# The last 40 adaLN rows: multiplied on GpSimd and summed on ScalarE, in place of one VectorE instruction

## The chip, the cores and the metric

The kernel runs on one core of one Trainium2 chip. A core has five engines that take their instructions in order, each from its own queue, and wait for one another by semaphores: TensorE (PE: matrix multiplies, with the weight loads listed apart as PEld), VectorE (DVE), ScalarE (ACT), GpSimd (POOL) and SyncE (SP), which here issues the DMAs. Times are microseconds (us) on the device, for one execution of the whole kernel; the figure for a kernel is the median of its runs.

## The reference, cut to what matters

One block of a transformer for 256 tokens of width 2048, all in float32: an FFN, a mixer (differential attention beside a causal convolution), and a second FFN. Each of the three has a norm in front whose scale and shift come from a vector `c` (adaLN), and a gate behind.

```python
c_act = silu(c)                                       # 1 x 2048
ada = einsum('bd,de->be', c_act, w_ada) + b_ada       # 1 x 18432: nine vectors of 2048
sh1, sc1, g1, shm, scm, gm, sh2, sc2, g2 = split(ada, 9)
h = modulate(rms_norm(x, ffn1_norm), sh1, sc1)        # h * (1 + sc) + sh
x = x + 0.5 * g1 * swiglu(h, ffn1_w_gu, ffn1_w_down)
h = modulate(rms_norm(x, mix_norm), shm, scm)
x = x + gm * hybrid_mixer(h, ...)
h = modulate(rms_norm(x, ffn2_norm), sh2, sc2)
x = x + 0.5 * g2 * swiglu(h, ffn2_w_gu, ffn2_w_down)
```

`ffn1_w_gu` and `ffn2_w_gu` are 2048 x 11264, the `w_down` 5632 x 2048, `w_ada` is 2048 x 18432 (151 MB, the largest input).

## The kernel before, in words

**adaLN rows.** The 18432 outputs of the adaLN product are 144 "rows" of 128. A row is a tile of 128 partitions (its outputs) by 2048 elements (the input dimension), 1 MB. The function `ada(j)` (L185) loads row j into a buffer `raw` by a DMA on SP (L190), multiplies it by `c_bc`, the activated `c` on all partitions, and sums along the free axis into one column of `ada_cols` by one instruction on VectorE (L191); that instruction shows in the profile as two, CUSTOM_DVE_ANT_0 and DVE_READ_ACCUMULATOR2_ANT. After each odd row a small add puts the bias on two columns (L195). Rows 0 to 47 belong to the first FFN, 48 to 95 to the mixer, 96 to 143 to the second FFN. Within 48, 32 alternate scale and shift for the 16 blocks of the norm, and the last 16 are the gate. `modulation` (L226) turns a pair into the scale and shift for one block (L233), and calls for rows that haven't come yet; `gate` (L258) does so for the last 16.

**Weights.** `w_tile` (L286) loads a weight tile of 128 x 2048 (1 MB) into the same four `raw` buffers, on the same SP queue (L292). Each half of it is split in two: ScalarE casts it to `whi` (L303), VectorE subtracts to get the rest, `wlo` (L305). `whi` and `wlo` have four buffers each, that is two weight tiles. `mm3` (L324) makes a product out of three matmuls (L327, L331, L332).

**Second FFN.** `ffn` (L637) first runs stage A: for each of 22 column chunks it loads the weight tile for the first quarter of the input, multiplies it for both token halves, and ScalarE copies the accumulators away (L664). Its later tiles take the other three quarters, for which the norm's blocks 4 to 15 must be done (`piece`, `complete`, L425 and L438; instructions L447 to L452), and so rows 104 to 127. Between the tiles the code asks for rows: 0.78 of a row per tile in stage A up to row 128 (`ada_share`, L215, called at L655, L770 and L774), then 0.5 a tile up to row 144 (L859), with `ada_until` (L200) where a block's rows are due. The first call in the second FFN (L769) stands in `tc.issue_after(st.last.ins)`, which queues what it traces on the engine of that instruction, VectorE, behind it. Then come the tiles of the down product, in a Strassen-like form (L463), whose gate needs rows 128 to 143.

**Order.** In the source, loads, splits, matmuls and rows are only stated; a planner orders each engine's queue by the order of the source and its own estimate of what is ready, and puts in the semaphore waits. A DMA into a `raw` buffer waits until the buffer's last reader is done. GpSimd has little: memsets and the reciprocal roots of the norms (L152, an exponent of -0.5). Before the second FFN starts, the mixer's end adds the residual (L1334, L1335), sums squares (L358), takes the root (L152) and runs the first block of the norm (L384 to L403).

Of the kernel before, what the change touches and what calls it, by code (L numbers as in the profile page):

```python
# [20 lines left out]
AF = mybir.ActivationFunctionType  # L21
ALU = mybir.AluOpType
# [18 lines left out]
EXT = (1,) * 8 + (2,) * 4 + (3,) * 3  # L41
LOADS = [(0,), (1,), (2, 3), (4, 5), (6, 7)] + [(c,) for c in range(8, NCH)]
BY_TILE = 5
X_BEHIND = 2
AGAIN = [4, 5, 6]
EARLY = [[3, 8, 9], [4, 5, 6], [7, 10, 11], [12, 13, 14]]
# [34 lines left out]
def block_kernel(ctx: ExitStack, tc: tile.TileContext, x_in, pos_in, w_ada, small, w_gu1, w_dn1,  # L81
                 w_in, w_out, w_gu2, w_dn2, out):
    nc = tc.nc
# [14 lines left out]
    def nm(s):  # L98
        uid[0] += 1
        return f"{s}_{uid[0]}"  # L100
# [40 lines left out]
    c_bc = cbp.tile([P, D], F32, tag="c_bc", name="c_bc")  # L141
# [41 lines left out]
    ada_cols = {}  # L183

    def ada(j):  # L185
        g = j // 8
        if g not in ada_cols:
            ada_cols[g] = const.tile([P, 8], F32, name=f"ada{g}")
        raw = rawp.tile([P, D], F32, tag="raw", name=nm("raw"))
        nc.sync.dma_start(out=raw, in_=w_ada[j])  # L190
        nc.vector.tensor_tensor_reduce(out=raw, in0=raw, in1=c_bc, scale=1.0, scalar=0.0, op0=ALU.mult,  # L191
                                       op1=ALU.add, accum_out=ada_cols[g][:, j % 8:j % 8 + 1])
        if j % 2 == 1:
            p0, o = _COLS["bada"][0] + j - 1, j % 8 - 1
            nc.vector.tensor_add(out=ada_cols[g][:, o:o + 2], in0=ada_cols[g][:, o:o + 2], in1=cst[:, p0:p0 + 2])  # L195
# [4 lines left out]
    def ada_until(j):  # L200
        while ada_next[0] < j:
            ada(ada_next[0])
            ada_next[0] += 1
# [11 lines left out]
    def ada_share(r, limit):  # L215
        credit[0] += r
        while credit[0] >= 1.0:
            credit[0] -= 1.0
            if ada_next[0] < limit:
                ada(ada_next[0])  # L220
                ada_next[0] += 1
# [88 lines left out]
    def w_first(cs, held):  # L310

        n = len(cs)
        raw = blk([P, 2, 512])
        w_dma[0] = nc.sync.dma_start(out=raw[:, :n, :], in_=w_gu1[cs[0]:cs[0] + n, 0].rearrange("c p n -> p c n")[:, :, :512])
        hi = blk([P, 2, 512], F32R) if held else whp.tile([P, 2, 512], F32R, tag="whi", name=nm("whi"))
        lo = blk([P, 2, 512], F32R) if held else wlp.tile([P, 2, 512], F32R, tag="wlo", name=nm("wlo"))

        def split():
            nc.scalar.copy(out=hi[:, :n, :], in_=raw[:, :n, :])  # L319
            nc.vector.tensor_sub(out=lo[:, :n, :], in0=raw[:, :n, :], in1=hi[:, :n, :].bitcast(F32))  # L320

        return [lambda j, i=i: (hi[:, i, :], lo[:, i, :]) for i in range(n)], split
# [314 lines left out]
    def ffn(st, w_gu, w_dn, gate_base, ada_a, ada_b, nxt, again, early, early_3):  # L637
# [37 lines left out]
        if not st.done:  # L675
# [4 lines left out]
            def load(i):  # L680
                cs = LOADS[i]
                if ext[cs[0]] == 1:
                    views, split = w_first(cs, X_BEHIND < i < BY_TILE)
                    ws.update(zip(cs, views))
                    if i < BY_TILE:
                        return split
                    split()
                else:
                    ws[cs[0]] = w_tile(w_gu[cs[0], 0], False, (0, ext[cs[0]]), ext[cs[0]] < 4)

            def begin_ready():
                while begun[0] < 4 and base + 2 * begun[0] + 2 <= ada_next[0]:
                    st.tile(st.raws[begun[0]], tmp([P, S]), (begun[0], slice(0, S)))
                    begun[0] += 1
# [10 lines left out]
            split = []  # L705
            for i in range(BY_TILE):
                split.append(load(i))
                if i == X_BEHIND:
                    with tc.issue_after(w_dma[0].ins):
# [7 lines left out]
            def products(i, t):  # L717
                for c in LOADS[i]:
                    acc = acc_tile()
                    mm3(acc, act(0, t), ws[c](0), True, True, i > 0 and t == 0)  # L720
                    if parts[c] is None:
                        parts[c] = blk([P, NT, 512])
                    last_part[0] = nc.scalar.copy(out=parts[c][:, t, :], in_=acc)

            with tc.manual_schedule(engines={mybir.EngineType.Activation, mybir.EngineType.DVE, mybir.EngineType.PE}):
# [17 lines left out]
                products(4, 0)  # L743
                for i in range(BY_TILE):
                    products(i, 1)
                    if i == 2:
                        load(BY_TILE)
                    if i == 3:
                        begin_ready()
            for i in range(BY_TILE, len(LOADS) + AHEAD):  # L750
                if i < len(LOADS):
# [704 lines left out]
```

## Time and profile before the change

| | |
|---|---|
| median of 3 runs | 1838.04 us (1837.12 to 1838.94) |
| the profiled execution, first to last instruction (its span; it has no other time) | 1835.9 us |
| TensorE busy | 1812.0 us |
| VectorE busy | 1521.8 us |
| ScalarE busy | 960.7 us |
| GpSimd busy | 28.3 us, 29 instructions |
| L191, the 142 whole rows on VectorE | 324.1 us, 2.28 us each |

A row of the timeline gives the start and the duration in us, the engine, the line of the kernel, the operation, the tiles it writes and reads, their shapes and a count (x2 where neighbours are merged); in square brackets stands how long the engine had been idle before it, and what it had waited for. A row of a group gives the total in us, the mean of one in ns, and the idle time ahead. A row of waits gives who waited for whom: the total in us, how often, and the longest. A row of windows gives the stretch and its length, then busy time and number of instructions (x) for each engine, the granted clock of TensorE, the busy share of the DMA engines and GB/s; where it is asked for one line alone, that line's engine only. A line like "min/median/max" gives durations in ns.

### The profile page before, as it was taken

Reading aid. Unit: us, or ns where it says so; the run is one execution under the profiler, and the core shown is the slowest. Engines: PE = TensorE matmul, PEld = TensorE weight load, DVE = VectorE, ACT = ScalarE, POOL = GpSimd, SP = SyncE. Lnnn points to the kernel's source line nnn. Section 1 sums busy time; section 2 is a strip of 40 time slices with the busy share of each in tenths; the row PEclk is TensorE's granted clock in tenths of the full one; section 3 lists DMA queues with packets and bytes.
Section 4 is the critical chain, followed back from the end, with each engine's and each line's share of the span. In section 5 each row is a group of like instructions: output and inputs, shape, how many; then the busy total and the mean of one; then the engine's idle time right before and its main releaser. Section 6 shows DMA issues by size and latency. Waiting matters only on the chain.

```text
span 1835.9 us, 22042 instructions
## 1 busy us (share of the span) xinstructions
PE 1812.0 (99%) x8205; PEld 1493.1 (81%) x8205; DVE 1521.8 (83%) x2018; ACT 960.7 (52%) x1477; POOL 28.3 (2%) x29
## 2 busy tenths in 40 slices
PE   7999999999999999999999999999999999999998
PEld 5788888888888887888888788888888888888887
DVE  7889869999888787898999768878877755699877
ACT  6554344444444343566798646664444444455453
POOL 0000000000000000000110000000000000000000
PEclk9999999999999999999999999999999999999999
DMA  9988978889899888765544467899777755555552
GB/s 375 352 307 300 352 272 301 343 306 340 336 322 357 353 343 329 289 256 187 181 159 161 161 229 294 315 335 339 263 273 284 285 197 188 184 206 208 205 210 111
DMA packets 72731, 495.93 MB, mean 270 GB/s; under 512 B 8192, under 2 KB 8624, under 8 KB 15152
## 3 DMA queue, kind: packets, MB, share of 16 engines
q1 hardware_dynamic: 72624, 494.53, 72.2%
q8 instruction: 64, 1.05, 0.2%
q14 instruction: 43, 0.35, 0.1%
HBM read 492.37 MB, written 2.12 MB: 269 GB/s over the span
## 4 chain that ended last, share of the span: by engine, by line
PE 90%; DVE 5%; ACT 2%; issue 1%; DMA 1%; POOL 0%; SPq 0%; POOLq 0%; DVEq 0%; ACTq 0%
PE acc L331 28%; PE acc L332 28%; PE acc L327 28%; DVE wlo L305 2%; PE tp L836 1%; PE tp L332 1%; PE tp L331 1%; PE tp L327 1%; DMA blk<-in_w_gu_dram 1%; PE acc L1123 1%; DVE blk L1015 1%; ACT whi L303 0%; PE tp L392 0%; DMA blk<-in_w_ada_dram 0%; DVE wlo L511 0%
## 5 line engine op out<-in xcount | busy, mean ns | idle before, releaser
L303 ACT CAST whi<-raw 128x1024 fp32r<-128x1024 f32 (+1 forms) x581 | 599.8, 1045 | 610.8 <-PE acc L332 450.3
L331 PE MATMUL acc<-wlo,blk 128*128 128x512 f32 x2340 | 913.5, 390 | 5.8 <-DVE wlo L305 5.8
L327 PE MATMUL acc<-whi,blk 128*128 128x512 f32 x2343 | 913.3, 393 | 1.7 <-ACT blk L401 1.3
L332 PE MATMUL acc<-whi,blk 128*128 128x512 f32 x2340 | 912.5, 390 | 0.1
L305 DVE TENSOR_TENSOR wlo<-raw,whi 128x1024 fp32r<-128x1024 f32 (+1 forms) x581 | 692.6, 1210 | 210.3 <-ACT whi L303 208.8
L331 PEld LDWEIGHTS acc<-wlo,blk 128*128 128x128 f32 x2340 | 439.6, 188 | 99.4 <-DVE wlo L305 10.3
L327 PEld LDWEIGHTS acc<-whi,blk 128*128 128x128 f32 x2343 | 440.0, 188 | 92.8 <-ACT blk L401 1.7
L332 PEld LDWEIGHTS acc<-whi,blk 128*128 128x128 f32 x2340 | 439.3, 188 | 92.4 <-DVE blk L403 0.7
L191 DVE CUSTOM_DVE_ANT_0 raw<-raw,c_bc 128x2048 f32<-128x2048 f32 x142 | 324.1, 2284 | 9.0 <-DMA raw<-in_w_ada_dram 8.8
L510 ACT CAST whi<-raw 128x1024 fp32r<-128x1024 f32 (+1 forms) x56 | 53.0, 946 | 70.2 <-PE tp L332 31.9
L511 DVE TENSOR_TENSOR wlo<-raw,whi 128x1024 fp32r<-128x1024 f32 (+1 forms) x56 | 60.9, 1088 | 19.0 <-ACT whi L510 18.7
L664 ACT COPY blk<-acc 128x512 f32<-128x512 f32 x72 | 41.9, 589 | 60.6 <-PE acc L332 57.9
L1015 DVE SCALAR_TENSOR_TENSOR blk<-blk,cst,blk 128x245 f32<-128x245 f32 (+21 forms) x176 | 70.5, 456 | 0.6 <-ACT blk L1013 0.5
L828 DVE TENSOR_TENSOR blk<-acc,blk 128x512 f32<-128x512 f32 x88 | 56.8, 682 | 0.2
L327 PE MATMUL acc<-blk,blk 128*128 128x512 f32 x104 | 41.3, 400 | 1.0 <-ACT blk L319 1.0
L332 PE MATMUL acc<-blk,blk 128*128 128x512 f32 x100 | 39.0, 392 | 0.0
L331 PE MATMUL acc<-blk,blk 128*128 128x512 f32 x100 | 39.0, 390 | 0.0
L830 DVE TENSOR_TENSOR blk<-blk 128x256 f32<-128x256 f32 x88 | 33.3, 417 | 0.7 <-ACT blk L829 0.7
L829 ACT ACTIVATE blk<-blk 128x256 f32<-128x256 f32 x88 | 32.2, 411 | 2.1 <-DVE blk L828 2.1
L349 DVE TENSOR_TENSOR blk<-tp,blk 128x512 fp32r<-128x512 f32 x44 | 29.9, 684 | 1.6 <-ACT blk L348 1.6
L305 DVE TENSOR_TENSOR blk<-raw,blk 128x1024 fp32r<-128x1024 f32 x24 | 28.8, 1218 | 0.8 <-ACT blk L303 0.8
L450 ACT ACTIVATE tmp<-tp,ada,scales 128x128 f32<-128x128 f32 x36 | 14.8, 459 | 28.0 <-DVE scales L233 15.5
(223 smaller groups left out, 1023.5 us busy)
## 6 DMA issues: line engine op xcount, KB each, us to landing
raw<-in_w_gu_dram SPq DMA_DIRECT2D x161, 1024.0 KB, 5.3
raw<-in_w_ada_dram SPq DMA_DIRECT2D x142, 1024.0 KB, 6.3
raw<-in_w_dn_dram SPq DMA_DIRECT2D x88, 1024.0 KB, 5.2
raw<-in_w_in_dram SPq DMA_DIRECT2D x40, 1024.0 KB, 4.8
raw<-in_w_out_dram SPq DMA_DIRECT2D x16, 1024.0 KB, 4.8
raw<-in_w_gu_dram SPq DMA_DIRECT2D x8, 768.0 KB, 6.0
blk<-in_w_gu_dram SPq DMA_DIRECT2D x10, 512.0 KB, 14.5
blk<-gate_line SPq DMA_DIRECT2D x6, 512.0 KB, 4.9
```

The costliest lines, as they stand in the source:

```text
L191: nc.vector.tensor_tensor_reduce(out=raw, in0=raw, in1=c_bc, scale=1.0, scalar=0.0, op0=ALU.mult, op1=ALU.add, accum_out=ada_cols[g][:, j ...
L303: nc.scalar.copy(out=hi[:, :m, :], in_=rw)
L305: nc.vector.tensor_sub(out=lo[:, :m, :], in0=rw, in1=hi[:, :m, :].bitcast(F32))
L327: nc.tensor.matmul(acc, ah, wh, start=start, stop=False)
L331: nc.tensor.matmul(acc, ah, wl, start=False, stop=False)
L332: return nc.tensor.matmul(acc, al, wh, start=False, stop=stop)
L510: nc.scalar.copy(out=hi[:, :n, :], in_=src)
L511: nc.vector.tensor_sub(out=lo[:, :n, :], in0=src, in1=hi[:, :n, :].bitcast(F32))
L664: last_part[0] = nc.scalar.copy(out=parts[c][:, t, :], in_=accs[t])
L828: nc.vector.tensor_add(out=p[:, t, :], in0=accs[t], in1=p[:, t, :])
L830: nc.vector.tensor_mul(out=p[:, t, 256:], in0=p[:, t, :256], in1=p[:, t, 256:])
L1015: nc.vector.scalar_tensor_tensor(out=y[:, d:], in0=u, scalar=w, in1=y[:, d:], op0=ALU.mult, op1=ALU.add)
```

## The change

For rows 104 to 143, the two lines of VectorE's multiply-and-sum become a GpSimd multiply of the whole tile in place, and a copy on ScalarE, also in place, whose accumulator gives the sum along the free axis. Rows up to 103 stay as they were. The bias add stays on VectorE, and the load stays where it was.

```diff
+ON_POOL = 104
...
         raw = rawp.tile([P, D], F32, tag="raw", name=nm("raw"))
         nc.sync.dma_start(out=raw, in_=w_ada[j])
-        nc.vector.tensor_tensor_reduce(out=raw, in0=raw, in1=c_bc, scale=1.0, scalar=0.0, op0=ALU.mult,
-                                       op1=ALU.add, accum_out=ada_cols[g][:, j % 8:j % 8 + 1])
+        dst = ada_cols[g][:, j % 8:j % 8 + 1]
+        if j < ON_POOL:
+            nc.vector.tensor_tensor_reduce(out=raw, in0=raw, in1=c_bc, scale=1.0, scalar=0.0, op0=ALU.mult,
+                                           op1=ALU.add, accum_out=dst)
+        else:
+            nc.gpsimd.tensor_tensor(out=raw, in0=raw, in1=c_bc, op=ALU.mult)
+            nc.scalar.activation(out=raw, in_=raw, func=AF.Copy, accum_out=dst)
         if j % 2 == 1:
             p0, o = _COLS["bada"][0] + j - 1, j % 8 - 1
             nc.vector.tensor_add(out=ada_cols[g][:, o:o + 2], in0=ada_cols[g][:, o:o + 2], in1=cst[:, p0:p0 + 2])
```

## The prediction

> **What bounds the kernel now.** I read the page first, then busy time by stage, then the groups of VectorE and ScalarE in the stage that the change reaches, then the waits of TensorE and of the DMA queue, then single rows of the timeline.
>
> ```profile
> span 1835.9 us, 22042 instructions
> PE 1812.0 (99%) x8205; PEld 1493.1 (81%) x8205; DVE 1521.8 (83%) x2018; ACT 960.7 (52%) x1477; POOL 28.3 (2%) x29
> ```
> ```profile
> L191 DVE CUSTOM_DVE_ANT_0 raw<-raw,c_bc x40: 2277/2284/2293, 1115.4 to 1458.3; 128x2048 f32<-128x2048 f32 x40
> L191 DVE DVE_READ_ACCUMULATOR2_ANT ada<- x40: 77/82/85, 1117.6 to 1460.5; 128x1 f32 x40
> ```
> ```profile
> core 0: us, PE busy (x) PEld busy (x) DVE busy (x) ACT busy (x) POOL busy (x), PEclk, DMA share, GB/s
> 1115.00:1180.00 65.00, 65.00 (x295) 53.68 (x294) 54.92 (x64) 38.28 (x55) 0.00 (x0) 1.00 0.85 329
> 1180.00:1260.00 80.00, 80.00 (x356) 65.98 (x355) 66.89 (x76) 43.79 (x57) 0.00 (x0) 1.00 0.93 340
> 1260.00:1360.00 100.00, 100.00 (x458) 82.65 (x457) 80.95 (x96) 47.63 (x62) 0.00 (x0) 1.00 0.76 283
> 1360.00:1460.00 100.00, 100.00 (x454) 82.77 (x453) 78.11 (x90) 44.57 (x54) 0.00 (x0) 1.00 0.77 283
> ```
> ```profile
> PE tp L392 <- DVE tmp L384: 0.9, 2, 0.6
> ```
>
> The kernel is bound by TensorE, which is busy 99% of the span. The 40 rows that move are the ones multiplied between 1115 and 1460 us, in the second FFN; there TensorE is busy in every microsecond at the full granted clock (PEclk 1.00), and the last line is its only wait on another engine between 1100 and 1470 us: 0.9 us. VectorE is 80 to 85% busy there, yet it makes nothing late. So relief for VectorE has next to nothing to win: at most that 0.9 us. What decides is whether the new path of a row makes TensorE late. I count 0.2% of the time, 3.7 us, as the least that a measurement of this kernel can tell from no change.
>
> **What goes and what comes.** VectorE loses, for each row, 2.28 us of multiply-and-sum and 0.08 us of accumulator read: 40 x 2.37 = 95 us, none of it on the path to the end. Added are one GpSimd multiply of 128x2048 and one ScalarE pass with accumulator per row. The bias add (L195) stays on VectorE, but now waits for ScalarE. No DMA moves, but each row's buffer is released later.
>
> GpSimd's price. No row shows a large multiply on it; the nearest are these (the first line is a memset of one element per partition):
>
> ```profile
> 0.24 0.10 POOL L1446 MEMSET const-float32-0.0<- 128x1 f32 x1 [0.24 <-issue]
> 881.77 0.95 POOL L1064 MEMSET blk<- 64x1024 f32 x1
> 20.23 0.56 POOL L152 TENSOR_TENSOR rstd<-rstd,half 128x1 f32<-128x1 f32 x1 [8.82 <-DVE rstd L151]
> ```
>
> One stream costs (0.95 - 0.10) / 1023 = 0.83 ns an element, so 1.70 us for 2048, and the smallest two-operand instruction 0.56 us. The multiply has three streams, two read and one written: fully overlapped it is 0.56 + 1.70 = 2.3 us, with two in turn 4.0, all three in turn 5.7. I take 4.5, nearer to two in turn, because the memset row shows the write side alone and two operands have to come in beside it. The Trainium skill (GPSIMD Engine Reference, Elementwise — side-by-side cycle accounting) gives 4497 ns, measured, for an fp32 add of 2048 elements; no run here shows it yet, and by it the sum would be the one below.
>
> Whether it runs beside VectorE. The trace of before has GpSimd instructions that meet a VectorE instruction with two operands in SBUF:
>
> ```profile
> 998.19 1.21 DVE L305 TENSOR_TENSOR wlo<-raw,whi 128x1024 fp32r<-128x1024 f32 x1
> 998.36 1.92 POOL L152 TENSOR_TENSOR rs<-rs,half 128x4 f32<-128x4 f32 x1 [37.51 <-DVE rs L151]
> ```
> ```profile
> 1013.98 1.21 DVE L305 TENSOR_TENSOR wlo<-raw,whi 128x1024 fp32r<-128x1024 f32 x1
> 1014.15 1.91 POOL L152 TENSOR_TENSOR rs<-rs,half 128x4 f32<-128x4 f32 x1 [6.65 <-DVE rs L151]
> 1018.55 1.14 POOL L152 TENSOR_TENSOR rs<-rs,half 128x4 f32<-128x4 f32 x1 [2.49 <-DVE rs L151]
> ```
>
> The same 128x4 instruction takes 1.91 us in two cases and 1.14 us in a third. In both long cases it started 0.17 us after an L305 and ended 0.88 us after that L305 ended (998.19 + 1.21 = 999.40, against 1000.28; 1015.19 against 1016.06). So a VectorE instruction that reads two SBUF operands holds GpSimd off until it is done. The other direction can't be seen, since these GpSimd instructions read almost nothing; its bounds are that a multiply holds VectorE off for 0 us and for its whole 4.5. I take the whole: it is the same pair of instructions wanting the same way into the memory, and nothing shown makes the way divisible. The Trainium skill (SBUF — State Buffer, Who interferes with whom) states just this rule: a VectorE instruction with two SBUF inputs and a GpSimd instruction that reads SBUF shut each other out, whichever starts first, for the whole instruction. The trace agrees for VectorE first (0.88 us both times); GpSimd first, no run here shows, and without the rule the sum would be that of the first rival.
>
> **The sum, 1115 to 1260 us (145 us).** These are VectorE's groups there, and its L191 time by stage:
>
> ```profile
> L305 DVE TENSOR_TENSOR wlo<-raw,whi 128x1024 fp32r<-128x1024 f32 x52 | 61.5, 1220 | 20.7 <-ACT whi L303 20.7
> L191 DVE CUSTOM_DVE_ANT_0 raw<-raw,c_bc 128x2048 f32<-128x2048 f32 x22 | 50.1, 2283 | 0.0
> L784 DVE TENSOR_TENSOR blk<-acc,blk 128x512 f32<-128x512 f32 x6 | 3.8, 681 | 0.0
> L447 DVE TENSOR_SCALAR tmp<-tp,scales,ada 128x128 f32<-128x128 f32 x10 | 3.6, 406 | 1.9 <-PE tp L392 1.8
> ```
> ```profile
> 1115.00:1180.00 65.00, 25.05 (x22) 1.00 0.85 329
> 1180.00:1260.00 80.00, 25.21 (x22) 1.00 0.93 340
> 1260.00:1360.00 100.00, 20.18 (x17) 1.00 0.76 283
> 1360.00:1460.00 100.00, 20.50 (x19) 1.00 0.77 283
> ```
>
> VectorE is busy 54.9 + 66.9 = 121.8 us, of which L191 is 50.3, so 71.5 us stay. Of these 7.4 us (L784 and L447) read PSUM and at most one SBUF tensor, and can run beside GpSimd; 64 us can't. The 22 rows need 22 x 4.5 = 99 us of GpSimd. What excludes each other is 64 + 99 = 163 us in a stage of 145: 18 us too much. At 2.3 us a multiply it is 115 us and fits; at 4.0 it is 152 (7 over); at 5.7 it is 189 (44 over).
>
> How much of that is hidden:
>
> ```profile
> 1128.02 1.27 ACT L664 COPY blk<-acc 128x512 f32<-128x512 f32 x2 [2.83 <-PE acc L332]
> 1129.19 2.00 ACT L303 CAST whi<-raw 128x1024 fp32r<-128x1024 f32 x2
> 1130.27 2.36 DVE L305 TENSOR_TENSOR wlo<-raw,whi 128x1024 fp32r<-128x1024 f32 x2 [0.97 <-ACT whi L303]
> 1133.46 1.27 ACT L664 COPY blk<-acc 128x512 f32<-128x512 f32 x2 [2.28 <-PE acc L332]
> ```
>
> A weight tile takes TensorE 5.44 us (from one L664 pair to the next). The halves split at 1130.27 to 1132.63 are for the tile that TensorE begins about when the next L664 pair starts, at 1133.5: VectorE is ahead by some 2 us for the first half and, as the second half is wanted 2.7 us later, 3.6 us for the second. That lead, 3 us, is paid back once. So the stage grows by 18 - 3 = 15 us, all of it TensorE waiting for L305.
>
> From 1260 to 1460 us: VectorE 159.1 - 40.7 = 118.4 us without L191, and 18 rows x 4.5 = 81; together 199.4 of 200 even if everything excludes. It fits; I count 0, and at 5.7 us a multiply (221 us) up to 20.
>
> The first rows.
>
> ```profile
> 1081.58 24.36 SPq L190 DMA_DIRECT2D raw<-in_w_ada_dram  x3
> ```
>
> The first of them is loaded from 1081.6 us on, yet multiplied only at 1115.4 (row of L191), because the code (L769) queues the multiply behind the last norm instruction, which is VectorE's. GpSimd isn't VectorE, so a multiply may start earlier and hold up the residual adds or the reciprocal root (L152) between 1095 and 1110 us, where TensorE does wait (the 0.9 us above); that costs 0 to 4.5 us, and it takes two multiplies out of the crowded stage, worth up to 9. I count 0.
>
> ScalarE. Its pass:
>
> ```profile
> L358 ACT ACTIVATION_READ_ACCUMULATOR tmp<-xall x20: 184/186/190, 6.7 to 1107.9; 128x1 f32 x20
> L451 ACT CAST blk<-tmp 128x512 fp32r<-128x512 f32 x4 | 2.4, 625 | 0.0
> L303 ACT CAST whi<-raw 128x1024 fp32r<-128x1024 f32 x52 | 52.4, 1050 | 12.4 <-DMA raw<-in_w_gu_dram 11.5 <-DVE ada L191 0.5 <-PE acc L332 0.3
> ```
>
> From 512 to 1024 elements the cast grows by 0.425 us, so 2048 are 1.05 + 0.85 = 1.9, with the accumulator read 2.1 us. In the stage ScalarE is busy 38.3 + 43.8 = 82.1; with 22 x 2.1 = 46 it is 128 of 145. It fits if it doesn't wait: 17 us are spare, 0.77 us a row.
>
> Forecast: 15 us on the profiled span, 1835.9 + 15 = 1851. The median of the three runs, 1838.04, is 2.1 us above that span, so the time is 1853 us.
>
> **Rivals.** First, not slower: GpSimd yields, or holds VectorE only while it starts. Then VectorE drops to 71.5 of 145 us, ScalarE has its 17 us to spare, a later row costs nothing, and the time stays at 1838, no more than 1 us below. For it: no row shows VectorE held off, and at under 3.7 us a multiply (64 + 22 x 3.7 = 145) everything fits even under full exclusion. That is the point from which it decides. Against: the rows at 998 and 1014. Chance 0.24, of which 0.02 for over 0.2% faster.
>
> Second, the queue of ScalarE. The pass waits for the multiply, and behind it in order stand the accumulator copies (L664) and the casts of the next tile. If the planner puts it so that ScalarE waits half a multiply, 2.25 us, a row, 22 x (2.25 - 0.77) = 33 us are added, in place of the 15: 1871. It decides from 0.77 us of wait a row. For it: ScalarE's spare time lies in a 2.3 us gap per tile ahead of L664, hardly over the 2.1 us that the pass takes. Against: ScalarE waits for DMA or VectorE before its casts for 12 us in this stage without TensorE noticing. Chance 0.12.
>
> Third, the four load buffers.
>
> ```profile
> SPq L292 <- DVE ada L191: 106.3, 23, 6.2
> ```
>
> Weight loads wait for rows' buffers to come free: 106 us over 23 loads between 1100 and 1470 us. A row will hold its buffer 4.5 + 2.1 - 2.37 = 4.2 us longer, and the load that takes the buffer next starts that much later.
>
> ```profile
> raw<-in_w_gu_dram SPq DMA_DIRECT2D x63, 1024.0 KB, 6.0
> ```
> ```profile
> 1204.92 0.33 SPq L292 DMA_DIRECT2D raw<-in_w_gu_dram  x1
> ```
> ```profile
> 1213.67 1.99 ACT L303 CAST whi<-raw 128x1024 fp32r<-128x1024 f32 x2
> ```
>
> A load issued at 1204.92 lands 6.0 us later, at 1210.9, and is cast at 1213.67: 2.8 us to spare. 4.2 - 2.8 leaves 1.4 us late; for half of the 22 rows' loads that is 15 us, less the 3 us of lead 12: 1850. It decides from a hold of 2.8 us more, that is from a multiply of 3.1 us. For it: ScalarE waits 11.5 us for such landings already (row of L303). Against: landing gets shorter where loads are spread out. Chance 0.10. The forecast has 0.54.
>
> **How the numbers follow.** Slower is forecast, second and third rival: 0.76. Same is 0.22, faster 0.02. The low end is no change less 1 us, 1837. The high end is a multiply of 5.7 us: 44 - 3 = 41 us over, 1879, which also takes in the second rival at 1871; beyond lies the sum of 5.7 us with ScalarE waiting or the 20 us later on, about 0.1.
>
> **What would show it.** GpSimd has 40 multiplies of 4 to 5 us, longer where an L305 was ahead. L305 no longer takes 1.22 us in all cases: those that met a multiply are recorded longer or follow idle time put down to GpSimd. TensorE's waits for L305, now absent from 1100 to 1470 us, come to over 10 us, nearly all before the 24th row is done; the stretch from there to the end keeps its length. The forecast is wrong if L305 stays at 1.22 us and starts on time beside running multiplies, if TensorE's waits come from ScalarE's copies and casts while VectorE is idle (second rival), or if the casts wait for DMA (third).

## The result and the profile after

| | before | after |
|---|---|---|
| median of 4 runs | 1838.49 us (1837.12 to 1839.46) | 1919.68 us (1916.6 to 1923.86) |
| ratio, 95% interval | | 1.0447 [1.0432, 1.0463] |
| span of the profiled execution | 1835.9 us | 1918.9 us |
| mean granted clock of TensorE | 0.999 | 0.985 |

The kernel is 81 us slower; 15 were forecast, and the top of the range was 1879. In the kernel after, the lines of the helpers stand six further down (L305 is L311, L303 is L309, L384 is L390, L664 is L670, L828 is L834), the GpSimd multiply is L197, the ScalarE sum L198, the bias add L201.

The page of after, span and busy time:

```profile
span 1918.9 us, 22125 instructions
PE 1838.6 (96%) x8205; PEld 1505.3 (78%) x8205; DVE 1530.6 (80%) x1938; ACT 1034.3 (54%) x1557; POOL 222.1 (12%) x69
```

The span grew by 83.0 us. TensorE is busy 1838.6 - 1812.0 = 26.6 us longer with the same 8205 matmuls, and idle 56.4 us longer. VectorE was relieved of 40 rows, 95 us, and is yet busy 8.8 us longer. These are its groups, and the new ones, between 1084 and 1600 us (after the bar: busy us, mean ns of one, then idle time ahead); the first two lines are the bias add and the norm's L384 in the kernel before, the rest is from after:

```profile
L195 DVE TENSOR_TENSOR ada<-ada,cst 128x2 f32<-128x2 f32 x20 | 3.1, 156 | 0.3
L384 DVE TENSOR_SCALAR tmp<-xall,rstd 128x512 f32<-128x512 f32 x2 | 1.0, 486 | 1.3 <-POOL rstd L152 1.3
```
```profile
L311 DVE TENSOR_TENSOR wlo<-raw,whi 128x1024 fp32r<-128x1024 f32 x144 | 241.5, 1702 | 118.0 <-ACT whi L309 118.0
L337 PE MATMUL acc<-wlo,blk 128*128 128x512 f32 x576 | 233.7, 406 | 31.9 <-DVE wlo L311 31.9
L197 POOL TENSOR_TENSOR raw<-raw,c_bc 128x2048 f32<-128x2048 f32 x40 | 192.9, 4823 | 296.0 <-DMA raw<-in_w_ada_dram 242.4 <-DVE wlo L311 39.6 <-ACT blk L835 9.6
L198 ACT ACTIVATE raw<-raw 128x2048 f32<-128x2048 f32 x40 | 76.6, 1916 | 136.1 <-POOL raw L197 136.1
L201 DVE TENSOR_TENSOR ada<-ada,cst 128x2 f32<-128x2 f32 x20 | 9.5, 474 | 36.0 <-ACT raw L198 36.0
```

The split into low halves has a mean of 1.70 us where it had 1.22; the bias add, 0.16 us before, has 0.47; a multiply takes 4.82; ScalarE stands 136 us waiting for multiplies, 3.4 us a row. TensorE's waits in the same stretch (total, times, longest):

```profile
PE acc L337 <- DVE wlo L311: 31.9, 17, 4.5
PE tp L398 <- DVE tmp L390: 8.9, 2, 8.6
PE acc L338 <- DVE blk L409: 6.0, 2, 3.5
PE tp L842 <- DVE blk L355: 4.9, 1, 4.9
PE acc L333 <- ACT whi L309: 3.4, 4, 1.6
```

With a last one of 2.1 us for a ScalarE cast of the norm they come to 57.2 us (0.9 before), which is about TensorE's whole new idle time; 51.7 of it is for VectorE. The first loss is at the residual add and the norm, in the timeline of after:

```profile
1088.79 9.34 POOL L197 TENSOR_TENSOR raw<-raw,c_bc 128x2048 f32<-128x2048 f32 x2 [47.25 <-DMA raw<-in_w_ada_dram]
...
1095.43 3.25 DVE L1341 TENSOR_TENSOR xall<-xall,tmp 128x512 f32<-128x512 f32 x1
...
1101.76 4.50 POOL L197 TENSOR_TENSOR raw<-raw,c_bc 128x2048 f32<-128x2048 f32 x1
1101.83 4.71 DVE L390 TENSOR_SCALAR tmp<-xall,rstd 128x512 f32<-128x512 f32 x1 [0.67 <-POOL rstd L153]
1106.69 1.08 PE L398 MATMUL tp<-cst,tmp 128*128 128x128 f32 x4 [8.62 <-DVE tmp L390]
```

The residual add L1341 takes 0.69 us elsewhere in that stage; here it ends at 1098.68, 0.55 us behind the pair of multiplies (1088.79 + 9.34 = 1098.13). The norm's L390 took 0.49 us before; here it starts 0.07 us after a multiply and ends 0.28 us after it. TensorE waits 8.62 us for it. Later in stage A, the same timeline:

```profile
1174.06 5.11 POOL L197 TENSOR_TENSOR raw<-raw,c_bc 128x2048 f32<-128x2048 f32 x1 [0.42 <-issue]
1175.70 3.48 DVE L201 TENSOR_TENSOR ada<-ada,cst 128x2 f32<-128x2 f32 x1 [0.99 <-ACT raw L198]
...
1179.30 2.36 DVE L311 TENSOR_TENSOR wlo<-raw,whi 128x1024 fp32r<-128x1024 f32 x2
1180.58 0.79 PE L337 MATMUL acc<-wlo,blk 128*128 128x512 f32 x1 [2.45 <-DVE wlo L311]
...
1185.55 4.60 POOL L197 TENSOR_TENSOR raw<-raw,c_bc 128x2048 f32<-128x2048 f32 x1 [6.38 <-DVE wlo L311]
1190.18 1.92 ACT L198 ACTIVATE raw<-raw 128x2048 f32<-128x2048 f32 x1 [5.20 <-POOL raw L197]
1190.81 4.62 POOL L197 TENSOR_TENSOR raw<-raw,c_bc 128x2048 f32<-128x2048 f32 x1 [0.66 <-DMA raw<-in_w_ada_dram]
...
1192.22 3.23 DVE L201 TENSOR_TENSOR ada<-ada,cst 128x2 f32<-128x2 f32 x1 [6.72 <-ACT raw L198]
1192.56 2.00 ACT L309 CAST whi<-raw 128x1024 fp32r<-128x1024 f32 x2
```

Read it downwards. A bias add of two columns, 0.16 us of work, is held until the multiply ends (1174.06 + 5.11 = 1179.17; the add ends at 1179.18); the low halves behind it in VectorE's queue start late, and TensorE stands for 2.45 us. Then ScalarE stands 5.20 us for a multiply, with the accumulator copies and the casts of the next tile behind it, and VectorE 6.72 us for ScalarE's sum; that done, the next bias add meets the next multiply.

TensorE's clock in these microseconds (windows of after; the number behind the last (x) is the granted clock):

```profile
1160.00:1165.00 5.00, 4.99 (x21) 3.49 (x19) 2.17 (x1) 3.87 (x6) 1.09 (x1) 1.00 0.30 98
1180.00:1184.00 4.00, 3.42 (x8) 2.75 (x9) 2.52 (x3) 4.00 (x6) 0.00 (x0) 0.50 0.57 229
1184.00:1187.00 3.00, 3.00 (x9) 2.28 (x9) 1.50 (x2) 0.64 (x2) 1.45 (x1) 0.53 0.99 401
1187.00:1190.00 3.00, 3.00 (x15) 2.45 (x14) 0.00 (x0) 0.00 (x0) 3.00 (x1) 1.00 0.85 350
```

After the gap of 2.45 us, which ends at 1180.58, the clock is half until about 1186.8. In the rows of TensorE a matmul then has 0.63 us and starts 0.43 after the one before (1181.17, 1181.60, 1182.02), where it normally has 0.39 and 0.23:

```profile
1181.17 0.63 PE L338 MATMUL acc<-whi,blk 128*128 128x512 f32 x1
1181.60 0.63 PE L333 MATMUL acc<-whi,blk 128*128 128x512 f32 x1
...
1186.99 0.39 PE L337 MATMUL acc<-wlo,blk 128*128 128x512 f32 x1
1187.22 0.40 PE L338 MATMUL acc<-whi,blk 128*128 128x512 f32 x1
```

That is the other part of the loss: (0.999 - 0.985) x 1918.9 = 27 us, the 26.6 us that TensorE is busy longer. The length of a gap alone doesn't decide it. These are three more gaps:

```profile
1136.76 0.50 PE L338 MATMUL acc<-whi,blk 128*128 128x512 f32 x1 [2.46 <-DVE blk L409]
1483.97 0.80 PE L337 MATMUL acc<-wlo,blk 128*128 128x512 f32 x1 [2.32 <-DVE wlo L311]
1522.72 0.50 PE L337 MATMUL acc<-wlo,blk 128*128 128x512 f32 x1 [2.33 <-DVE wlo L311]
```

Behind the second the clock is 0.50 for 3.1 us; in the 3.2 us behind the first and the third it is 1.00. Three half-clock stretches begin while matmuls run, at about 1128.7, 1282.4 and 1446.3 us (there the spacing of the matmuls goes from 0.23 to 0.43 us), and end about 3.4 us later; the distances, 153.7 and 163.9 us, are 45 and 48 steps of 3.41 us. Other ends lie on the same grid (1186.8, 1251.7 and 1306.1 are 16, 35 and 51 steps behind the end at 1132.1). So in this trace the clock changes on a fixed grid, which would explain why gaps of the same length cost differently: it matters where in the grid they fall.

By stage: the first and the last start of three lines that every tile passes, first in before, then in after (min/median/max duration in ns, then the two starts):

```profile
L664 ACT COPY blk<-acc x44: 577/589/610, 1109.0 to 1228.2; 128x512 f32<-128x512 f32 x44
L784 DVE TENSOR_TENSOR blk<-acc,blk x6: 676/680/684, 1233.6 to 1244.8; 128x512 f32<-128x512 f32 x6
L828 DVE TENSOR_TENSOR blk<-acc,blk x44: 678/681/692, 1283.3 to 1598.7; 128x512 f32<-128x512 f32 x44
```

```profile
L670 ACT COPY blk<-acc x44: 567/588/636, 1119.1 to 1272.0; 128x512 f32<-128x512 f32 x44
L790 DVE TENSOR_TENSOR blk<-acc,blk x6: 677/680/682, 1281.2 to 1303.1; 128x512 f32<-128x512 f32 x6
L834 DVE TENSOR_TENSOR blk<-acc,blk x44: 676/681/692, 1340.9 to 1681.8; 128x512 f32<-128x512 f32 x44
```

The first tile is 10.1 us late; stage A's 44 copies take 33.7 us more (152.9 against 119.2); up to the last L790 another 14.5 are added (58.3 late); the stretch from the first to the last L834 takes 25.5 more (340.9 against 315.4). With -0.7 between, the sum is 83.1, and nothing is added or regained behind.

### The profile page after: what moved, and what is told of

Same layout as the page of the kernel before. It is cut to its first block, busy times and chain, and to the rows that moved or that the text cites. A ratio compares the mean times of both kernels' runs of the same rounds, so it can differ in the third digit from the quotient of the medians.

```text
span 1918.9 us, 22125 instructions
## 1 busy us (share of the span) xinstructions
PE 1838.6 (96%) x8205; PEld 1505.3 (78%) x8205; DVE 1530.6 (80%) x1938; ACT 1034.3 (54%) x1557; POOL 222.1 (12%) x69
## 4 chain that ended last, share of the span: by engine, by line
PE 72%; DVE 10%; DMA 5%; issue 4%; ACT 4%; POOL 4%; POOLq 0%; SPq 0%; ACTq 0%; DVEq 0%
PE acc L337 23%; PE acc L338 23%; PE acc L333 22%; DVE wlo L311 6%; DMA raw<-in_w_ada_dram 4%; POOL raw L197 3%; ACT whi L309 2%; PE tp L338 1%; PE tp L337 1%; PE tp L333 1%; PE tp L842 1%; DMA blk<-in_w_gu_dram 1%; PE acc L1129 1%; DVE blk L1021 1%; ACT raw L198 0%
## 5 line engine op out<-in xcount | busy, mean ns | idle before, releaser
L311 DVE TENSOR_TENSOR wlo<-raw,whi 128x1024 fp32r<-128x1024 f32 (+1 forms) x581 | 760.1, 1329 | 248.3 <-ACT whi L309 246.6
L309 ACT CAST whi<-raw 128x1024 fp32r<-128x1024 f32 (+1 forms) x581 | 596.1, 1044 | 510.9 <-PE acc L338 373.9
L194 DVE CUSTOM_DVE_ANT_0 raw<-raw,c_bc 128x2048 f32<-128x2048 f32 x102 | 233.0, 2285 | 12.3 <-DMA raw<-in_w_ada_dram 12.1
L197 POOL TENSOR_TENSOR raw<-raw,c_bc 128x2048 f32<-128x2048 f32 x40 | 192.9, 4823 | 296.0 <-DMA raw<-in_w_ada_dram 242.4
L198 ACT ACTIVATE raw<-raw 128x2048 f32<-128x2048 f32 x40 | 76.6, 1916 | 136.1 <-POOL raw L197 136.1
L516 ACT CAST whi<-raw 128x1024 fp32r<-128x1024 f32 (+1 forms) x56 | 53.0, 946 | 70.2 <-PE tp L338 31.9
L517 DVE TENSOR_TENSOR wlo<-raw,whi 128x1024 fp32r<-128x1024 f32 (+1 forms) x56 | 60.9, 1087 | 19.0 <-ACT whi L516 18.7
L670 ACT COPY blk<-acc 128x512 f32<-128x512 f32 x72 | 40.6, 590 | 32.0 <-PE acc L338 30.8
L834 DVE TENSOR_TENSOR blk<-acc,blk 128x512 f32<-128x512 f32 x88 | 56.6, 682 | 0.0
L201 DVE TENSOR_TENSOR ada<-ada,cst 128x2 f32<-128x2 f32 x71 | 17.4, 245 | 36.8 <-ACT raw L198 36.0
L153 POOL TENSOR_TENSOR rs<-rs,half 128x8 f32<-128x8 f32 (+1 forms) x12 | 19.3, 1604 | 231.3 <-DVE rs L152 231.3
L333 PE MATMUL acc<-blk,blk 128*128 128x512 f32 x104 | 42.2, 409 | 0.6 <-ACT blk L325 0.6
L836 DVE TENSOR_TENSOR blk<-blk 128x256 f32<-128x256 f32 x88 | 42.2, 516 | 0.0
```

Of the source, the lines that this page charges most:

```text
L197: nc.gpsimd.tensor_tensor(out=raw, in0=raw, in1=c_bc, op=ALU.mult)
L198: nc.scalar.activation(out=raw, in_=raw, func=AF.Copy, accum_out=dst)
L309: nc.scalar.copy(out=hi[:, :m, :], in_=rw)
L311: nc.vector.tensor_sub(out=lo[:, :m, :], in0=rw, in1=hi[:, :m, :].bitcast(F32))
L333: nc.tensor.matmul(acc, ah, wh, start=start, stop=False)
L516: nc.scalar.copy(out=hi[:, :n, :], in_=src)
```

## The experiments

Each time is that of one run, beside one of the kernel before on the same chip; the difference is to that one (the first line has the medians of four runs each). These single runs of before lie between 1836.75 and 1839.74 us, so a difference of 3 us can't be told from none. The theories came in three steps: first, whether GpSimd's exclusion of VectorE or the longer path of a row costs the time; when neither did by itself, which link of the path the exclusion needs. The mean is that of the low-half split (1.22 us before) and "low halves" TensorE's wait for it (0.0 before), both between 1084 and 1600 us.

| run | us (before) | difference | mean, us | low halves, us |
|---|---|---|---|---|
| the change itself | 1919.68 (1838.49) | +81.2 | 1.70 | 31.9 |
| e1 multiply, no ScalarE sum | 1913.87 (1837.98) | +75.9 | 1.63 | 34.9 |
| e2 memsets for the multiply, with sum | 1841.61 (1837.98) | +3.6 | 1.23 | 0.2 |
| e3 memsets, no sum | 1840.57 (1837.98) | +2.6 | 1.23 | 0.0 |
| e4 multiply on VectorE, with sum | 1847.01 (1837.98) | +9.0 | 1.22 | 2.0 |
| e5 sum queued late | 1914.37 (1837.56) | +76.8 | 1.77 | 30.3 |
| e6 multiply in four pieces | 1922.19 (1837.56) | +84.6 | 1.47 | 22.6 |
| e7 gate rows only (16) | 1863.11 (1837.56) | +25.6 | 1.35 | 9.1 |
| e8 from row 108 on (36) | 1916.69 (1837.56) | +79.1 | 1.68 | 42.9 |
| e9 free multiplies, four pieces | 1846.49 (1839.74) | +6.8 | 1.46 | 4.6 |
| e10 no multiplies | 1842.79 (1839.74) | +3.1 | 1.22 | 0.0 |
| e11 memsets, sum queued late | 1838.63 (1839.74) | -1.1 | 1.22 | 0.7 |
| e12 memsets, casts behind the sum | 1841.66 (1839.74) | +1.9 | 1.22 | 1.3 |
| e13 held buffer only | 1913.76 (1836.75) | +77.0 | 1.76 | 33.5 |
| e14 queue only | 1944.43 (1836.75) | +107.7 | 1.26 | 17.3 |
| e15 free multiplies, whole | 1848.65 (1839.34) | +9.3 | 1.71 | 5.4 |
| e16 held buffer, four pieces | 1918.49 (1839.34) | +79.1 | 1.70 | 50.5 |

### e1 to e4: the multiply or the path

e1, the multiply without ScalarE's pass:

```diff
-            nc.scalar.activation(out=raw, in_=raw, func=AF.Copy, accum_out=dst)
+            nc.gpsimd.tensor_tensor(out=dst, in0=raw[:, :1], in1=raw[:, :1], op=ALU.mult)
```

> Rows 104 to 143 keep GpSimd's multiply; ScalarE's sum is left out, a GpSimd instruction of one element per partition writes the row's column instead. Against 1838.5 us before and 1919.7 after (81 us apart). Exclusion between GpSimd and VectorE: nearly all stays, 55 us or more over before, since the multiplies are the same. ScalarE's queue: what waited behind the sums waits no longer, 25 us or less over before. Load buffers: a row's buffer is held 2.1 us less of 4.2 us more, about 40 us over.

e2, the path without GpSimd reading anything: memsets of about the same length, then the pass.

```diff
-            nc.gpsimd.tensor_tensor(out=raw, in0=raw, in1=c_bc, op=ALU.mult)
+            nc.gpsimd.memset(raw, 0.5)
+            nc.gpsimd.memset(raw, 0.25)
+            nc.gpsimd.memset(raw[:, :1280], 0.5)
```

> The multiply is replaced by memsets of the same buffer on GpSimd, two of 2048 and one of 1280 elements, some 4.5 us in all, that only write; the sum on ScalarE stays, so the product is left out. Exclusion (two operands read against GpSimd's reads): mostly gone, 30 us or less over before. ScalarE's queue: it waits for GpSimd as long as in the changed kernel, 60 to 85 us over. Load buffers: held as long, 60 to 85 us over.

e3, both edits at once:

> Both at once: memsets in place of the multiply, and no sum on ScalarE (product and sum are left out). Exclusion and ScalarE's queue both say under 10 us over before. Load buffers alone: a row's buffer is still held 2.2 us longer than before, so 20 to 40 us over.

e4, `nc.vector` in place of `nc.gpsimd` in the multiply:

> The same work without GpSimd: VectorE multiplies the last 40 rows, ScalarE sums them. Exclusion: nothing to exclude, under 5 us over before. ScalarE's queue: the sums still stand in it, but the product comes 2.3 us sooner and is on time more often, 10 to 40 us over. Load buffers: held 2.1 us longer than before, 10 to 40 us over.

Measured: +75.9, +3.6, +2.6 and +9.0. The groups of e2:

```profile
L339 PE MATMUL acc<-wlo,blk 128*128 128x512 f32 x690 | 268.7, 389 | 0.2 <-DVE wlo L313 0.2
L313 DVE TENSOR_TENSOR wlo<-raw,whi 128x1024 fp32r<-128x1024 f32 x173 | 210.6, 1225 | 178.6 <-ACT whi L311 178.3
L200 ACT ACTIVATE raw<-raw 128x2048 f32<-128x2048 f32 x40 | 76.7, 1918 | 14.0 <-POOL raw L199 14.0
```

GpSimd works 1.81 + 1.81 + 1.17 = 4.8 us on each row, as long as a multiply takes; the sum, and behind it the next load into the buffer, still wait for it, and it costs 3.6 us. The splits keep their 1.22 us: these GpSimd instructions, which only write, do not hold VectorE off. So the longer path costs next to nothing here, and ScalarE's pass isn't needed for the loss (e1). Two limits: ScalarE waits only 14.0 us for GpSimd in e2, not the change's 136.1 that its forecast took for granted, and the planner's order isn't quite the same, with most sums one or two casts further back in ScalarE's queue. VectorE's own multiply ahead of ScalarE's pass (e4) costs 9.0, far less than GpSimd's, though more than the 5 us that exclusion as the only cause allowed.

### e5 to e8: can the loss be moved

e5 states the sum one row late and queues it behind the last cast, so that ScalarE finds the product done:

```diff
-            nc.scalar.activation(out=raw, in_=raw, func=AF.Copy, accum_out=dst)
+            unsummed.append((j, raw, dst))
+            sum_rows(144, 1)
...
+            with tc.issue_after(last_cast[0].ins):
+                nc.scalar.activation(out=raw, in_=raw, func=AF.Copy, accum_out=dst)
```

> The changed kernel with one thing moved: a row's sum on ScalarE and its bias add are stated only when the next row is asked for, and the sum is queued behind the casts of the weight tile stated last, about one tile later. In the changed kernel ScalarE waits 136 us for GpSimd in front of the sums; here it should wait under 30. Exclusion by itself (rereading and shutting out, whatever the queues): stays 50 us or more over before. Queues behind a late product (a planner that takes the multiply for shorter than it is, so that copies and casts stand behind a sum that waits): 30 us or less over before. Load buffers: a row's buffer is held some 5 us longer still, so as slow as the changed kernel or slower, 80 us over or more.

e6 cuts the multiply, so that VectorE can come in between:

```diff
-            nc.gpsimd.tensor_tensor(out=raw, in0=raw, in1=c_bc, op=ALU.mult)
+            for q in range(0, D, 512):
+                nc.gpsimd.tensor_tensor(out=raw[:, q:q + 512], in0=raw[:, q:q + 512], in1=c_bc[:, q:q + 512], op=ALU.mult)
```

> The multiply in four instructions of 512 elements, everything else as in the changed kernel. If the two engines shut each other out for a whole instruction, a VectorE instruction waits some 1.2 us at most instead of 4.6, though the time shut out in all stays: by throughput alone (163 us of work that excludes itself in 145) still 50 us or more over before; if the length of one shut-out is what hurts, because it outlasts the 2 to 3.6 us by which VectorE is ahead, 30 us or less over. Queues behind a late product: no change, 70 us or more over.

e7 has `ON_POOL = 128`, e8 `ON_POOL = 108`:

> Only rows 128 to 143 go to GpSimd (the bound of 104 becomes 128). In the changed kernel this stretch grew by about 25 us. Exclusion as summed in the prediction (199 of 200 us): 0 to 5 us over before. If single shut-outs hurt even where the sum fits: 15 to 30 us over.

> Rows 104 to 107 stay on VectorE (the bound becomes 108), so that nothing of GpSimd meets the end of the mixer. The first copy of stage A (L664 before, L670 after) came 10 us late in the changed kernel. Early multiplies as the cause of that: 12 to 20 us less than the changed kernel, with the first copy where it was before. Otherwise 36 of 40 rows remain and it gains 4 of 40 of 81 us, 8 us.

Measured: +76.8, +84.6, +25.6, +79.1. In e5 ScalarE waits for GpSimd only 1.8 us in all, and the loss stays; another wait has taken its place (waits of e5):

```profile
ACT whi L327 <- DMA raw<-in_w_gu_dram: 95.1, 33, 6.9
```

The casts now wait 95 us for weight tiles that land late (14.6 us over 5 times before). Those loads in turn wait mostly until a split gives its buffer back (194.4 us over 41 loads, the longest 10.6, where before had 176.8 over 47, the longest 5.1) and hardly for a row's sum (14.0 us); which delay came first isn't shown. In e6 the pieces take 1.62 us each, 6.5 a row against 4.8 whole: VectorE does come in between (mean 1.47), and the product comes later for it, ScalarE waiting 167.6 us. The loss goes with the number of rows, 1.6 us a row in e7, 2.2 in e8, 2.0 in the change, so already 16 rows, where the forecast had counted nothing, are not free. In e8 the norm's first block is undisturbed and the first copy starts at 1108.9 as before, yet +79.1 remains, inside the scatter of the change's own four runs (1916.6 to 1923.86 us); 8 us less, or 12 to 20, had been expected. What is saved at the boundary is lost later.

### e9 to e12: exclusion without waiting, waiting without exclusion

e9 lets GpSimd multiply as much, on data at hand and into columns that nobody reads, while VectorE releases the row at once:

```diff
-            nc.gpsimd.tensor_tensor(out=raw, in0=raw, in1=c_bc, op=ALU.mult)
-            nc.scalar.activation(out=raw, in_=raw, func=AF.Copy, accum_out=dst)
+            nc.vector.tensor_tensor(out=dst, in0=raw[:, :1], in1=raw[:, :1], op=ALU.mult)
+            mark = cst[:, s0 + 512 + j - ON_POOL:s0 + 513 + j - ON_POOL]
+            nc.vector.tensor_tensor(out=mark, in0=dst, in1=dst, op=ALU.mult)
+            nc.gpsimd.tensor_tensor(out=scrap[:, :1], in0=mark, in1=mark, op=ALU.mult)
+            for q in range(0, D, 512):
+                nc.gpsimd.tensor_tensor(out=scrap, in0=c_bc[:, q:q + 512], in1=c_bc[:, q:q + 512], op=ALU.mult)
```

> Exclusion by itself. Rows 104 to 143 are loaded and let go after one VectorE instruction of one element per partition, so product and sum are left out; when a row has come, GpSimd multiplies the same amount, four times 128x512, out of c_bc into a column block that nobody reads. No engine and no buffer waits for GpSimd. If shutting out costs by itself, through VectorE's late halves: 40 us or more over before. If it needs the chain (a sum that waits, a buffer held longer): 15 us or less over, since VectorE has no queue behind it but its own.

e10 keeps only the first of these added lines:

> The same without the multiplies: the last 40 rows are loaded and let go after one element (product and sum left out). The bound of what relief of VectorE could bring. All theories: 1837 to 1838, no more than 1 us less than before.

e11 is e5 with the memsets of e2 for the multiply; e12 is e2 with each cast queued behind the last sum (`with tc.issue_after(last_sum[0].ins)`):

> The kernel of the moved sum with write-only memsets in place of the multiply (product left out): buffers held as long as there by plan, 5 us longer than in the changed kernel, with no operand read by GpSimd. Load buffers held too long as the cause: 40 us or more over before, near the 77 us of the moved sum. Exclusion as the cause: 10 us or less over.

> Write-only memsets in place of the multiply (product left out), and on ScalarE the casts of every weight tile stated after a row are queued behind that row's sum, so that they stand behind a sum which waits for GpSimd. ScalarE's queue as the cause: 40 us or more over before. Exclusion as the cause: 10 us or less over.

Measured: +6.8, +3.1, -1.1, +1.9. With the rows' work taken from VectorE and given to nobody, nothing is gained (e10, a little above the 1838 us that all theories had as the most): relief is worth nothing here. With exclusion but nobody waiting, VectorE loses (1.464 - 1.222) x 172 = 42 us on its splits and the kernel 7. With ScalarE forced to wait 38.9 us for GpSimd and no exclusion (e12), 2; the change's wait of 136.1 us without exclusion was not reached by any run. Each half alone, as far as these runs go, costs little; the change has both and costs 81.

### e13 to e16: which wait the exclusion needs

e13: GpSimd multiplies the row in place, and only the next load into its buffer waits for that.

```diff
-            nc.gpsimd.tensor_tensor(out=raw, in0=raw, in1=c_bc, op=ALU.mult)
-            nc.scalar.activation(out=raw, in_=raw, func=AF.Copy, accum_out=dst)
+            nc.vector.tensor_tensor(out=dst, in0=raw[:, :1], in1=raw[:, :1], op=ALU.mult)
+            nc.gpsimd.tensor_tensor(out=raw[:, 1:], in0=raw[:, 1:], in1=c_bc[:, 1:], op=ALU.mult)
```

> GpSimd multiplies each of the 40 rows in place, but for its first column; VectorE's column comes from one element of the raw row, so the rows' sums are left out. No instruction of ScalarE or VectorE waits for GpSimd any more; only the load that takes the row's buffer next does. Theory A (exclusion costs time through the load buffers, whose release waits for GpSimd): 60 to 85 us slower than before, with ScalarE's casts waiting 50 us or more for weight loads and TensorE 20 us or more for the low halves of L305. Theory B (it costs time through the in-order queues of ScalarE and VectorE that wait for GpSimd): at most 15 us slower, as the free multiplies were (+6.8). Theory C (each of the two is enough): as A here.

e14 is e9 with one line more:

```diff
+            nc.scalar.activation(out=scrap, in_=scrap, func=AF.Copy, accum_out=dst)
```

> The free multiplies again (four of 128x512 for each of the 40 rows, on data at hand, the row's buffer released by a one-element instruction of VectorE; the rows' products are left out), and then a ScalarE pass of 128x512 with accumulator over GpSimd's result, into the row's column, for which the bias add waits. So ScalarE's and VectorE's queues wait for GpSimd and no buffer does. Theory A (load buffers): at most 20 us slower than before. Theory B (queues): 60 to 85 us slower, with TensorE waiting 20 us or more for the low halves. Theory C (each is enough): 60 us or more here and in the run with the held buffer.

Measured: +77.0 and +107.7, so both were slow. e14 does not answer what it was made for. Its group of ScalarE sums:

```profile
L205 ACT ACTIVATE cst<-cst 128x512 f32<-128x512 f32 x40 | 25.2, 631 | 221.5 <-POOL cst L204 221.5
```

Its multiplies start only when VectorE has come to the row, not when the row has landed, so ScalarE stands 5.5 us a row instead of the change's 3.4, and VectorE, starved of casts, meets few multiplies (mean 1.26). It shows that a long wait of ScalarE's queue is enough to cost time, not that the change's shorter one would be. In e13 the low halves are waited for as theory A said (33.5 us), but its other sign didn't come: the casts wait 26.1 us for weight loads, not 50. And e13 differs from e9 in two things, the buffer and the length of one multiply. So e15 is e9 with one whole multiply, and e16 is e13 with four pieces:

```diff
+            nc.gpsimd.tensor_tensor(out=c_bc[:, :1], in0=mark, in1=mark, op=ALU.mult)
+            nc.gpsimd.tensor_tensor(out=c_bc, in0=c_bc, in1=c_bc, op=ALU.subtract if j == ON_POOL else ALU.mult)
```

> As the free multiplies (the row's buffer released by a one-element instruction of VectorE, the rows' products left out, nobody waiting for GpSimd), but each row's work on GpSimd is one multiply of 128x2048 in place of four of 128x512. Theory L (what costs is the length of one instruction: VectorE is held off for up to 5 us at a time, more than its lead over TensorE, whoever waits for the product): 50 to 80 us slower than before, with the mean of L305 at 1.6 us or more in the second FFN and TensorE waiting over 15 us for the low halves. Theory C (exclusion costs only where something waits for GpSimd): at most 15 us slower.

> As the run with the held buffer alone (the load that takes the row's buffer next is all that waits for GpSimd, the rows' sums are left out), but with the row multiplied as four instructions of 128x512. Theory L (length of one instruction): at most 20 us slower than before. Theory C (a held buffer together with exclusion): 50 to 80 us slower, as with the whole multiply (+77.0).

Measured: +9.3 and +79.1. The groups of e15, then of e13, then of e16:

```profile
L315 DVE TENSOR_TENSOR wlo<-raw,whi 128x1024 fp32r<-128x1024 f32 x171 | 288.0, 1705 | 85.3 <-ACT whi L313 84.9
L341 PE MATMUL acc<-wlo,blk 128*128 128x512 f32 x680 | 265.7, 391 | 5.4 <-DVE wlo L315 5.4
L202 POOL TENSOR_TENSOR c_bc<-c_bc 128x2048 f32<-128x2048 f32 x40 | 160.9, 4022 | 3.1
```

```profile
L311 DVE TENSOR_TENSOR wlo<-raw,whi 128x1024 fp32r<-128x1024 f32 x149 | 257.8, 1758 | 56.5 <-ACT whi L309 54.0 <-PE acc L338 2.4
L337 PE MATMUL acc<-wlo,blk 128*128 128x512 f32 x589 | 238.2, 404 | 33.6 <-DVE wlo L311 33.5
L198 POOL TENSOR_TENSOR raw<-raw,c_bc 128x2047 f32<-128x2047 f32 x40 | 198.4, 4964 | 281.3 <-DMA raw<-in_w_ada_dram 126.0 <-DVE ada L197 64.7 <-DVE xall L1341 46.4
```

```profile
L312 DVE TENSOR_TENSOR wlo<-raw,whi 128x1024 fp32r<-128x1024 f32 x146 | 243.9, 1700 | 40.9 <-ACT whi L310 40.6
L338 PE MATMUL acc<-wlo,blk 128*128 128x512 f32 x581 | 236.7, 407 | 50.5 <-DVE wlo L312 50.5
```

The split has about the same mean in e15 and e13, 1.71 and 1.76 us; VectorE loses (1.705 - 1.222) x 171 = 83 us on it in e15. Where nothing waits for GpSimd, TensorE waits 5.4 us for the low halves and the kernel loses 9.3; where a load buffer is held until the multiply is done, 33.5 and 77.0. Cutting the multiply changes neither (6.8 against 9.3, 79.1 against 77.0).

The split isn't all that VectorE loses, so its busy time over the whole kernel is the fairer measure. e10, without multiplies, has 1441.7 us; e13 has 1592.8, 151 more, and e15 1543.3, of which 6 are its 40 added instructions, so 95 more. The two are not equal in exclusion. But the change is equal to e15: 1530.6 us against 1438.7 in e2, which has the same VectorE instructions, so 92 lost, and the kernel pays 81 us where e15 pays 9.3. And e6 loses only 1490.3 - 1438.7 = 52 and pays 84.6. So it isn't the amount of exclusion, nor the length of one instruction: exclusion needs something that waits for GpSimd, and a held load buffer is enough.

How the held buffer makes TensorE late can be read best in e16. The SP queue's waits for buffers, then VectorE's wait for its rows, both between 1050 and 1600 us:

```profile
SPq L299 <- POOL raw L199: 179.7, 28, 9.2
```

```profile
DVE ada L197 <- DMA raw<-in_w_ada_dram: 84.7, 15, 8.0
```

Weight loads stand 179.7 us for GpSimd to give buffers back (50.9 in e3, where the memsets hold them), so what is loaded behind them lands late, and VectorE, which takes its instructions in order, stands 84.7 us at its one-element instruction for a row (14.1 over 8 times in e15), with the splits of the next tile behind it. In e13 it is 30.7 us, and more of the loss seems to lie in meetings with the longer multiplies (one of these instructions, 0.15 us by itself, takes 4.57 at 1138.84). In e5 it is ScalarE's casts that stand, 95.1 us, in the change ScalarE's sums, 136.1. That the cause is one and the same behind these different queues is argued, not shown.

What stays open: how the loss divides between late loads and meetings in each of them, and how much the planner's order, which isn't the same in each run, adds. Whether exclusion with ScalarE's queue alone, at the change's 3.4 us a row, would have been enough is open too. More load buffers, or buffers of their own for the rows, would separate it further; neither was tried.

## Why the prediction was wrong

**What bounds the kernel, and what relief is worth: right.** TensorE makes the time, and e10, with the rows' work gone from VectorE (1441.7 us busy, 1521.8 before), is not faster than before (+3.1).

**The price of a multiply: right.** 4.5 us was taken; undisturbed it has 4.50 to 4.62 (rows at 1101.76, 1185.55 and 1190.81), 4.82 in the mean. No row had given that figure: the working came to 4.0 or 5.7, and 4.5 was chosen between them, so the rows alone would have left the size open. The estimate of ScalarE's pass, 1.9 us and 2.1 with the read of the accumulator, was 1.92 and 2.10.

**Exclusion with GpSimd first: right, and wider than taken.** The rows at 1095, 1101, 1175 and 1192 us show VectorE held off to the end of a multiply. The forecast counted L305 and what else reads two large SBUF operands; it left out that an instruction of 0.16 us (L201) pays the whole multiply as well, 3.48 us at 1175.70. The Trainium skill (SBUF — State Buffer, Who interferes with whom) has the rule that the forecast used, and limits it to GpSimd instructions that read SBUF; the trace agrees on both sides, with a mean split of 1.70 us in the stage with multiplies and 1.23 in the one with memsets of the same length.

**The sum: the step that failed.** It said: "That lead, 3 us, is paid back once. So the stage grows by 18 - 3 = 15 us, all of it TensorE waiting for L305", and of 1260 to 1460 us "It fits; I count 0". That sum treats the stage as a throughput: so much work that excludes each other, so much time. As a throughput it came near. In e15, where exclusion does nothing but take VectorE's time, multiplies of 4.02 us make stage A's 44 copies last from 1108.4 to 1234.9, 7.3 us more than before, and the stretch of the gate rows (1294.1 to 1609.7) 0.2; the prediction's own line for 4.0 us says 7 over, 3 of them covered by the lead, and 0 later. But in the change the multiply isn't only work that excludes, it is a link in a chain: a load buffer, ScalarE's in-order queue and the bias add wait for it. As the traces read, late releases make late loads and late casts, these take the lead from the next split, and that one meets the next multiply with nothing in hand. The lead is paid not once: TensorE waits 17 times for low halves, up to 4.5 us each, 9 of them (11.3 us) after 1320 us; the later stretch grows by 25.5 us, forecast 0, and e7 with its 16 rows alone has +25.6. The chain from one link to the next is read, not tested; that exclusion and a held buffer are costly only together is tested (e15 and the memset runs against e13 and e16).

**The rivals were each priced alone.** The second, ScalarE's queue, and the third, the four load buffers, were given +33 in place of the 15 and +12, and chances of 0.12 and 0.10, as alternatives to exclusion. Alone, the path costs -1 to +4 us (e2, e3, e11, e12). They were no alternatives: exclusion together with a held buffer is enough for the loss, and in the change exclusion comes together with both. No case held the product of two causes that are nearly harmless one by one, and so the range ended at 1879.

**The first rows: wrong, in part.** They were counted at 0, with 0 to 4.5 of cost; the first copy is 10.1 us late, since two instructions were held off where one was thought of and the halved clock came on top. Without it (e8) the kernel is no faster than the change's own scatter, so this loss doesn't add to the rest.

**TensorE's clock: not in the prediction.** It cost 27 of the 83 us. A forecast that has TensorE idle for some us, many times, has to add the half-speed stretches that follow many of the gaps. The Trainium skill (TensorE: Matmul & The Clock Gate, Part 1: The HAM clock gate) gives half rate after an idle window of about 3.4 us, in windows that run freely, and for about as long until it is lifted. The trace agrees on the step, 3.41 us, and differs on the idle time: a gap of 2.32 us was enough (1483.97), while one of 2.46 was not (1136.76), and the half clock behind the gap of 2.45 lasted some 6 us.

## What to carry to other kernels

Before moving work to an engine that can exclude another, ask two questions together: what does it shut out, and who waits for its result? Each alone may be nearly free (at most 9 and 4 us in these runs), and the two at once were 76 to 85. The likely reason is that an instruction which holds a buffer and is itself delayed makes the next tile late, and with it the next collision more expensive. A sum of busy times shows whether it fits, but not what it costs when neither engine has a lead; and relief for an engine that makes nobody late is worth nothing, so such a move had only a downside here.

## What the hardware showed that was not expected

TensorE's granted clock halved after gaps of 2.32 and 2.45 us and didn't after gaps of 2.33 and 2.46; its changes lie on a grid of 3.41 us. In all, 56 us of idle time cost 83 us. A VectorE instruction of two columns by 128 partitions, 0.16 us, was held for 3.48 us by a GpSimd multiply, and so was one with a single large SBUF operand and a column (L390, 4.71 us for 0.49); L408, which reads PSUM, kept its 0.41 us (1123.19) inside a multiply that ran from 1122.71 to 1127.65. A GpSimd memset of 128x2048, which only writes, took 1.81 us and left VectorE's 1.22 us as they were.
